# Gathering the experts' tokens as whole rows of 4 KB in two DMAs

## The chip, the cores and the metric

One core of one Trainium2 chip. The time is device microseconds of one execution. The engines are named as the profile names them: PE is TensorE (PEld its weight loads), DVE VectorE, ACT ScalarE, POOL GpSimd, SP SyncE.

## The reference, cut to what matters

The whole computation is an encoder block over 256 + 512 tokens of width 1024: a dilated attention beside a state-space mixer, then the expert layer, then a gated embedding. The change is in the expert layer:

```python
def _expert_choice_ffn(h, w_router, w_gate, w_up, w_down):   # h: (t, 1024), t = 512 and t = 256
    cap = max(1, CAPACITY_FACTOR * t // N_EXPERTS)           # 64 and 32 tokens an expert
    aff = jax.nn.softmax((h @ w_router).astype(jnp.float32), axis=-1)
    gate, idx = lax.top_k(aff.T, cap)                        # each of 16 experts chooses its tokens
    xs = h[idx]                                              # the gather
    def expert(args):
        xe, wg, wu, wd = args                                # (1024, 2816) twice, (2816, 1024)
        return (jax.nn.silu(xe @ wg) * (xe @ wu)) @ wd
    ye = lax.map(expert, (xs, w_gate, w_up, w_down)) * gate[..., None]
    return jnp.zeros_like(h).at[idx.reshape(-1)].add(ye.reshape(-1, h.shape[1]))   # the scatter
```

All of it is float32. The weights of 16 experts, 554 MB, are read once.

## The kernel before, in words

The kernel runs both groups of tokens (S, 512 of them; Q, 256) through the mixer and the router, then loops over 16 experts. An expert's 96 tokens stand in NB = 3 blocks of 32: two of S, one of Q.

**Layout of a block.** TensorE works in columns of 32: `blocks` (L1150) issues, for each block and each j of 0..3, a matmul with 32 stationary columns that writes 32 partitions of PSUM. The stationary operand of block b is `xts[e][b]`, 128 partitions x 256: partition 32 j + i holds features of the j-th quarter of a feature group, and the 32 columns of step k are the 32 tokens. To get there the normalized tokens are stored in DRAM (`hn_d`) with their features reordered in four quarters of 256 (L784), so that a quarter of a token is one run of 1 KB, row 4 t + j of `hn_d`.

**Gather and turn.** `quart` (L1108 to L1120) holds, for each block and expert, 128 row numbers 4 t + j. `gather(e)` (L1131) issues three indirect DMAs on POOL, one a block, each of which brings 128 runs of 1 KB to the 128 partitions of a buffer `xg0`, `xg1` or `xg2`. `turn_x(e)` (L1137) transposes each buffer in squares of 32 x 32 on DVE, 128x256 at once, into `xts`, which has two buffers a block. A buffer `xg` has one copy, so a gather waits until the transposes of the expert before have read it.

**The expert loop.** For each expert there are two halves r of the hidden width. `up(e, r)` (L1158) takes 16 weight tiles of 704 KB (gate and up in turn) into six PSUM banks, ACT and DVE evacuate them (`sg`, `hv`) and DVE transposes the result into `ht`. `down(e, r)` (L1173) takes 11 tiles of 512 KB. Their order is shifted: up(e,0), down(e-1,1), up(e,1), down(e,0), so that between two up phases there is always a down phase, in which the evacuation runs (but for the first expert, which has up(0,0) and up(0,1) back to back). After down(e,1) `emit` (L1205) scales with the gates and adds into DRAM with three indirect DMAs, the scatters. A scheduler that orders instructions by their dependences has put the transposes and the gather behind them at the evacuation of up(e,1), in the down phase of down(e,0), once an old `xts` is free.

**Weights.** `Feed` (L127) issues the 864 weight tiles on SP in the order of use into 25 slots; a slot is refilled when the last matmul on it is done, so SP waits for matmuls.

`PAD_L` and `PAD_R` are tiles that nothing uses: they set where in SBUF the pools behind them begin.

Of the kernel before, what the change touches and what calls it, by code (L numbers as in the profile page):

```python
# [10 lines left out]
F32 = mybir.dt.float32  # L11
BF16 = mybir.dt.bfloat16
F32R = mybir.dt.float32r
I32 = mybir.dt.int32
U32 = mybir.dt.uint32
AF = mybir.ActivationFunctionType
ALU = mybir.AluOpType
# [4 lines left out]
P = 128  # L22
D = 1024
# [8 lines left out]
NE = 16  # L32
CAPS = (64, 32)
NB = 3
FR = FF // 2
FC = FR // 4
DC = D // 4
# [129 lines left out]
def block_kernel(ctx, tc, x_prompt, x_sample, p_prompt, p_sample, rel_bias, g_mix, w_in, conv_w, conv_b, dt_bias,  # L167
                 a_log, d_skip, g_ssd, w_out, g_ffn, w_router, w_gate, w_up, w_down, g_pg, w_pg, w_ple, g_ple,
                 g_final, c_masks, c_table, c_rows, y_prompt, y_sample):
    nc, E = tc.nc, mybir.EngineType  # L170
    S, Q = Group(0), Group(1)

    def rows(prompt, sample, t):
        return prompt[t * P:(t + 1) * P, :] if t < 2 else sample[(t - 2) * P:(t - 1) * P, :]
# [1 line left out]
    x_rows = lambda t: rows(x_prompt[0], x_sample[0], t)  # L176
    p_rows = lambda t: rows(p_prompt[0, 0], p_sample[0, 0], t)
    N_B, N_C, N_D, PLE_A = 8, 11, 6, 4
    PAD_L, PAD_R = 88, 24
    y_rows = lambda t: rows(y_prompt[0], y_sample[0], t)  # L180

    def row_bcast(v, n):
# [2 lines left out]
    def pool(name, side):  # L185
        return tc.alloc_tile_pool(name=name, bufs=1, side=side, reuse_waits="tile")
# [36 lines left out]
    cpool = pool("consts", "left")  # L223
# [3 lines left out]
    dram = ctx.enter_context(tc.tile_pool(name="dram", bufs=1, space=DRAM))  # L227
    psum = ctx.enter_context(tc.tile_pool(name="psum", bufs=1, space=PSUM))

    def bank(tag, bufs):  # L230
        return psum.tile([P, 512], F32, tag=tag, bufs=bufs, name=tag)

    pA = lambda: bank("pA", 2)
    pB = lambda: bank("pB", 3)
# [5 lines left out]
    ident, u_le, u_ge, m_gt, m_lt, ones = (masks[:, i, :] for i in range(6))  # L240
# [6 lines left out]
    wr = cpool.tile([P, KD, NE], F32, name="wr")  # L247
    gates = cpool.tile([P, NB, NE], F32, name="gates")
    quart = cpool.tile([P, NB, NE], I32, name="quart")
    cpool.tile([P, PAD_L], F32, name="pad_l")  # L250

    tbl = dram.tile([H, 1024], F32, name="tbl")
    tbl_rep = dram.tile([H, P, 1024], F32, name="tbl_rep")
    for g in (S, Q):
        g.hn_d, g.acc_d = (dram.tile([4 * g.n, DC], F32, name=f"{x}{g.i}") for x in ("hn_d", "acc_d"))
        g.hn_rows, g.acc_rows = (x.rearrange("(t j) c -> t (j c)", j=4) for x in (g.hn_d, g.acc_d))


    latest, squares, halves_ = [], [], []
# [7 lines left out]
    def rstd_of(p, ss, n, width):  # L267
        r = p.tile([P, n], F32, tag="rstd", bufs=3, name="rstd")
        nc.vector.tensor_scalar(r, ss, 1.0 / width, EPS, op0=ALU.mult, op1=ALU.add)  # L269
        nc.gpsimd.tensor_tensor(r, r, mhalf[:, :n], op=ALU.pow)  # L270
        return r

    def sumsq(p, src, scr):
        ss = p.tile([P, 1], F32, tag="ss", bufs=3, name="ss")
        squares[:] = [nc.scalar.activation(scr, src, AF.Square, accum_out=ss)]
        return ss
# [759 lines left out]
    wk = pool("work", "right")  # L1036
# [6 lines left out]
    idx_u = wk.tile([32 + NE, CAPS[S.i]], U32, name="idxu")  # L1043
# [10 lines left out]
    at = pool("atts", "right")  # L1054
# [49 lines left out]
    sq, tq = slice(32, 32 + NE), slice(8 * FIRST_Q, 8 * ROUNDS)  # L1104
    p, p_q = pO(), pB()
    for u, x in enumerate((idx_u, vals)):
        reps = wk.tile([32 + NE, NB, 4, 32], F32, tag="reps", bufs=2, name="reps")
        nc.vector.tensor_copy(reps[:NE, :2], x[:NE].rearrange("p (b t) -> p b t", b=2).unsqueeze(2).to_broadcast(  # L1108
            [NE, 2, 4, 32]))
        nc.vector.tensor_copy(reps[sq, 2], x[sq, tq].unsqueeze(1).to_broadcast([NE, 4, 32]))  # L1110
        flat = reps.rearrange("p b j t -> p b (j t)")
        for b in range(2):
            nc.tensor.transpose(p[:, 32 * u + NE * b:32 * u + NE * (b + 1)], flat[:NE, b], ident[:NE, :NE])
        nc.tensor.transpose(p_q[:, NE * u:NE * (u + 1)], flat[sq, 2], ident[sq, sq])
        for y, src in ((slice(0, 2), p[:, 32 * u:32 * u + 32].rearrange("p (b e) -> p b e", b=2)),
                       (2, p_q[:, NE * u:NE * (u + 1)])):
            if u:
                nc.vector.tensor_copy(gates[:, y], src)
            else:
                nc.vector.tensor_scalar(quart[:, y], src, 4.0, rowc[:, 18:19], op0=ALU.mult, op1=ALU.add)  # L1120
    for _ in emb:
        pass
    w_a.release()
    w_c = pool("w_c", "left")
    exw = pool("experts", "left")
    of = (S, S, Q)
    xgs, xts, hts_, acc, pend = {}, {}, {}, {}, {}

    turned = []

    def gather(e):  # L1131
        xgs[e] = [exw.tile([P, DC], F32, tag=f"xg{b}", bufs=1, name="xg") for b in range(NB)]
        for b in range(NB):
            nc.gpsimd.indirect_dma_start(out=xgs[e][b], out_offset=None, in_=of[b].hn_d,  # L1134
                                         in_offset=bass.IndirectOffsetOnAxis(ap=quart[:, b, e:e + 1], axis=0))

    def turn_x(e):  # L1137
        xts[e] = [exw.tile([P, DC], F32, tag=f"x{b}", bufs=2, name="xe") for b in range(NB)]
        for b in range(NB):
            turned.append(nc.vector.transpose(xts[e][b], xgs[e][b]))  # L1140

    gather(0)
    wf.add(w_c, N_C)
    pw.release()
    w_d = pool("w_d", "right")
    wf.add(w_d, N_D)
    turn_x(0)


# [76 lines left out]
    for e in range(NE):  # L1226
        if e + 1 < NE:
            gather(e + 1)
        for r in range(2):
            up(e, r)  # L1230
            if r == 0 and e + 1 < NE:
                turn_x(e + 1)
                if 1 <= e <= NT:
                    ple_norm(e - 1)
            if e + r:
                down(e - 1 + r, 1 - r)
# [27 lines left out]
    for t in range(NT):  # L1264
        if t + 1 < NT:
            tail_prep(t + 1)
        xt, et, xh, xl, r = xs5.pop(t)
# [9 lines left out]
        r = rstd_of(wk, sumsq(wk, sg, q5.tile([P, D], BF16, tag="scr5", bufs=1, name="scr5")), 1, D)  # L1277
# [64 lines left out]
```

## Time and profile before

| | us |
|---|---|
| timed, median of 3 runs | 1941.67 |
| timed, lowest and highest | 1941.05, 1942.00 |
| profiled execution | 1953.96 |
| its span, first to last instruction | 1952.2 |
| PE busy in the span | 1908.5 |
| DVE, ACT, POOL busy | 476.2, 396.0, 280.4 |

The experts take the span from 476.5 us on (the first matmul of L1155) to 1862; before it are the mixer and router, behind it the gated embedding. In the page's 40 slices the DMA engines are at 9 of 10 from the tenth slice to the end of the experts and move 402 to 420 GB/s there; PE is at 9 throughout. Idle time of an engine that is not the bottleneck costs nothing, so the reading goes by what PE does from one half expert to the next. A line such as L1155 is the line of kernel.py that issued the instruction.

### The profile page before, as it was taken

To read this page: it belongs to the slowest core of one execution; us is meant where nothing else is said; L and a number is where in the kernel's file an instruction comes from. 1 tells how busy PE (TensorE), PEld (TensorE's weight loads), DVE (VectorE), ACT (ScalarE), POOL (GpSimd) and SP (SyncE) were. 2 spreads that over 40 slices of the span, in tenths; PEclk is the share of its full clock that TensorE was granted. 3 is DMA by queue.
4 is the path that set the end of the run, shared out by engine and by line. 5 is a ranking of instruction groups with operands and counts; after the bars stand their busy time and mean duration, and the time that the engine had idled before them with its cause. 6 is when DMAs were issued, how large, how long until landed. Compare 5 with 4: busy or idle time off the path is not lost.

```text
span 1952.2 us, 52796 instructions
## 1 busy us (share of the span) xinstructions
PE 1908.5 (98%) x23972; PEld 1525.3 (78%) x23972; DVE 476.2 (24%) x1002; ACT 396.0 (20%) x768; POOL 280.4 (14%) x278
## 2 busy tenths in 40 slices
PE   8999999998999999999999999999999999999988
PEld 7978988986688776788866668888888877777776
DVE  7767575735010000001100000010000000100144
ACT  6758645643000000000000000000000000000133
POOL 0342344222001011010101000010101000000110
PEclk9999999999999999999999999999999999999999
DMA  7553226267999999999999999999999999999821
GB/s 250 186 150 91 66 95 180 71 243 289 420 408 408 412 409 408 411 407 415 408 413 407 414 412 404 414 407 414 409 412 407 408 413 406 414 409 412 304 73 65
DMA packets 181601, 641.55 MB, mean 329 GB/s; under 512 B 21790, under 2 KB 56022, under 8 KB 181376
## 3 DMA queue, kind: packets, MB, share of 16 engines
q1 hardware_dynamic: 168108, 620.76, 79.9%
q0 software_dynamic: 13056, 17.31, 4.0%
q8 instruction: 188, 3.08, 0.6%
q14 instruction: 37, 0.30, 0.0%
q10 hardware_dynamic: 212, 0.09, 0.0%
HBM read 617.61 MB, written 19.96 MB: 327 GB/s over the span
## 4 chain that ended last, share of the span: by engine, by line
PE 90%; ACT 3%; DVE 3%; issue 2%; DMA 1%; POOL 0%; DVEq 0%; POOLq 0%; ACTq 0%
PE pA L1155 24%; PE pB L1155 23%; PE pT L1155 16%; PE pO L1155 8%; PE pA L263 5%; PE pA L264 5%; PE pA L265 5%; PE pO L702 2%; PE pT L693 1%; PE pT L281 1%; DVE ws L99 1%; DMA ws<-in_w_in 1%; ACT ws L98 1%; PE pB L790 0%; PE pB L685 0%
## 5 line engine op out<-in xcount | busy, mean ns | idle before, releaser
L1155 PE MATMUL pB<-wf,xe 128*32 128x352 f32 x6144 | 591.4, 460 | 6.0 <-DVE xe L1140 6.0
L1155 PE MATMUL pA<-wf,ht 128*32 128x256 f32 x8448 | 487.0, 379 | 3.1 <-issue 0.3
L1155 PEld LDWEIGHTS pA<-wf,ht 128*32 128x32 f32 x8448 | 395.3, 110 | 87.6 <-issue 20.4
L1155 PEld LDWEIGHTS pB<-wf,xe 128*32 128x32 f32 x6144 | 357.3, 110 | 118.2 <-DVE xe L1140 6.1
L1155 PE MATMUL pT<-wf,xe 128*32 128x352 f32 x4096 | 440.2, 460 | 0.0
L1170 DVE TENSOR_TENSOR hv<-sg,pT 128x352 f32<-128x352 f32 x64 | 32.1, 502 | 1232.7 <-PE pT L1155 1232.7
L1155 PEld LDWEIGHTS pT<-wf,xe 128*32 128x32 f32 x4096 | 244.7, 110 | 78.0 <-issue 2.2
L1155 PE MATMUL pO<-wf,xe 128*32 128x352 f32 x2048 | 287.1, 459 | 0.0
L1169 ACT ACTIVATE sg<-pB 128x352 f32<-128x352 f32 x96 | 44.6, 465 | 1091.2 <-PE pB L1155 1044.9
L1209 POOL DMA_INDIRECT acc_d<-ye,quart x48 | 75.5, 1574 | 730.4 <-ACT ye L1208 651.4
L1155 PEld LDWEIGHTS pO<-wf,xe 128*32 128x32 f32 x2048 | 131.3, 110 | 38.4 <-issue 0.4
L1134 POOL DMA_INDIRECT xg<-hn_d,quart x48 | 47.1, 981 | 300.9 <-DVE xe L1140 258.6
L99 DVE TENSOR_TENSOR ws<-ws 128x2048 fp32r<-128x2048 f32 (+1 forms) x31 | 68.5, 2214 | 39.2 <-ACT ws L98 38.8
L270 POOL TENSOR_TENSOR rstd<-rstd,mhalf 128x1 f32<-128x1 f32 (+1 forms) x36 | 22.9, 637 | 381.7 <-DVE rstd L269 381.7
L98 ACT ACTIVATE ws<-ws 128x2048 fp32r<-128x2048 f32 (+1 forms) x31 | 55.8, 1805 | 25.0 <-PE pA L264 13.0
L1208 ACT ACTIVATE ye<-pA,gates 128x256 f32<-128x256 f32 x48 | 19.4, 473 | 204.0 <-PE pA L1155 204.0
L265 PE MATMUL pA<-h,ws 128*128 128x512 f32 (+1 forms) x136 | 54.1, 398 | 1.2 <-DVE ws L99 1.2
L263 PE MATMUL pA<-h,ws 128*128 128x512 f32 (+1 forms) x136 | 54.7, 402 | 0.0
L264 PE MATMUL pA<-h,ws 128*128 128x512 f32 (+1 forms) x136 | 54.2, 398 | 0.0
L1171 DVE STREAM_TRANSPOSE ht<-hv 128x352 f32<-128x352 f32 x96 | 47.4, 519 | 0.6
L263 PE MATMUL pA<-wf,x 128*128 128x512 f32 x96 | 38.7, 403 | 6.7 <-ACT x L285 6.7
L263 PE MATMUL pA<-hq,ws 128*128 128x256 f32 (+1 forms) x136 | 40.0, 296 | 0.7 <-ACT xpq L382 0.7
(308 smaller groups left out, 2021.0 us busy)
## 6 DMA issues: line engine op xcount, KB each, us to landing
wf<-in_w_gate SPq DMA_DIRECT2D x256, 704.0 KB
wf<-in_w_up SPq DMA_DIRECT2D x256, 704.0 KB
wf<-in_w_down SPq DMA_DIRECT2D x352, 512.0 KB
ws<-in_w_in SPq DMA_DIRECT2D x24, 1024.0 KB
tbl_rep<-tbl SPq DMA_DIRECT2D x8, 512.0 KB
ws<-in_w_out SPq DMA_DIRECT2D x4, 1024.0 KB
wf<-in_w_pg SPq DMA_DIRECT2D x8, 512.0 KB
sk<-tbl_rep SPq DMA_DIRECT2D x8, 448.0 KB
```

Of the source, the lines that this page charges most:

```text
L98: self.nc.scalar.activation(hi, raw, AF.Copy)
L99: self.nc.vector.tensor_tensor(lo, raw, hi, op=ALU.subtract)
L263: nc.tensor.matmul(out, lhsT=sh, rhs=mh, start=first, stop=False)
L264: nc.tensor.matmul(out, lhsT=sh, rhs=ml, start=False, stop=False)
L265: latest[:] = [nc.tensor.matmul(out, lhsT=sl, rhs=mh, start=False, stop=last)]
L702: nc.tensor.matmul(po[:, c:c + HD], lhsT=pts[s - 3][j][:, k, :], rhs=g.v[:, k, h * HD:(h + 1) * HD], start=k == 0, stop=k == nt - 1)
L1134: nc.gpsimd.indirect_dma_start(out=xgs[e][b], out_offset=None, in_=of[b].hn_d, in_offset=bass.IndirectOffsetOnAxis(ap=quart[:, b, e:e + 1] ...
L1155: nc.tensor.matmul(out[b][32 * j:32 * j + 32], lhsT=st[b][:, 32 * k:32 * k + 32], rhs=w[:, j], start=first[b], stop=last, skip_group_check ...
L1169: nc.scalar.activation(sg, pg[b], AF.Silu)
L1170: nc.vector.tensor_tensor(hv, sg, pu[b], op=ALU.mult)
L1171: nc.vector.transpose(hts_[e, r][b], hv)
L1209: nc.gpsimd.indirect_dma_start(out=of[b].acc_d, out_offset=bass.IndirectOffsetOnAxis(ap=quart[:, b, e:e + 1], axis=0), in_=ye, in_offset=N ...
```

## The change

The tokens of experts 1 to 15 are fetched as whole rows of `hn_d` (4 KB a token) into one buffer `xg` of 128 x 1024, one token on a partition: rows 0 to 63 are the tokens of S, rows 64 to 95 those of Q. That takes two indirect DMAs, with the token numbers `token` as indices. The reordering in quarters that the three DMAs did is then done by the transposes: for block b and quarter j a 32x256 piece (partitions 32 b to 32 b + 31, columns 256 j on) goes to partitions 32 j to 32 j + 31 of `xts[e][b]`, four for each block, twelve for an expert. Expert 0 keeps the three DMAs by quarters and the three transposes, now into thirds of the same buffer's first 768 columns. `token` is made beside `quart`: the indices are cast to float (`ids`), transposed on PE and cast back. `hn_d` and `acc_d` are the same memory, declared by rows of 4 KB and viewed by quarters; the scatters are unchanged. `xg` grows from 3 KB to 4 KB a partition, and the pads are set anew.

```diff
-    PAD_L, PAD_R = 88, 24
+    PAD_L, PAD_R = 56, 88
...
+    token = cpool.tile([P, 2, NE], I32, name="token")
...
-        g.hn_d, g.acc_d = (dram.tile([4 * g.n, DC], F32, name=f"{x}{g.i}") for x in ("hn_d", "acc_d"))
-        g.hn_rows, g.acc_rows = (x.rearrange("(t j) c -> t (j c)", j=4) for x in (g.hn_d, g.acc_d))
+        g.hn_rows, g.acc_rows = (dram.tile([g.n, D], F32, name=f"{x}{g.i}") for x in ("hn_d", "acc_d"))
+        g.hn_d, g.acc_d = (x.rearrange("t (j c) -> (t j) c", j=4) for x in (g.hn_rows, g.acc_rows))
...
+    ids = wk.tile([32 + NE, CAPS[S.i]], F32, name="ids")
+    nc.vector.tensor_copy(ids[:NE], idx_u[:NE])
+    nc.vector.tensor_copy(ids[sq, :32], idx_u[sq, tq])
+    ps = pB(), pB()
+    nc.tensor.transpose(ps[0][:64, :NE], ids[:NE], ident[:NE, :NE])
+    nc.tensor.transpose(ps[1][:32, :NE], ids[sq, :32], ident[sq, sq])
+    for u, n in ((0, 64), (1, 32)):
+        nc.vector.tensor_scalar(token[:n, u], ps[u][:n, :NE], 1.0, None, op0=ALU.mult)
...
+    rows_of = ((S, slice(0, 64)), (Q, slice(64, 96)))
...
+    def fetch(out, src, at):
+        nc.gpsimd.indirect_dma_start(out=out, out_offset=None, in_=src,
+                                     in_offset=bass.IndirectOffsetOnAxis(ap=at, axis=0))
+
     def gather(e):
-        xgs[e] = [exw.tile([P, DC], F32, tag=f"xg{b}", bufs=1, name="xg") for b in range(NB)]
-        for b in range(NB):
-            nc.gpsimd.indirect_dma_start(out=xgs[e][b], out_offset=None, in_=of[b].hn_d,
-                                         in_offset=bass.IndirectOffsetOnAxis(ap=quart[:, b, e:e + 1], axis=0))
+        xgs[e] = exw.tile([P, D], F32, tag="xg", bufs=1, name="xg")
+        if e == 0:
+            for b in range(NB):
+                fetch(xgs[e][:, b * DC:(b + 1) * DC], of[b].hn_d, quart[:, b, e:e + 1])
+        else:
+            for g, r in rows_of:
+                fetch(xgs[e][r], g.hn_rows, token[:r.stop - r.start, g.i, e:e + 1])
 
     def turn_x(e):
         xts[e] = [exw.tile([P, DC], F32, tag=f"x{b}", bufs=2, name="xe") for b in range(NB)]
         for b in range(NB):
-            turned.append(nc.vector.transpose(xts[e][b], xgs[e][b]))
+            if e == 0:
+                turned.append(nc.vector.transpose(xts[e][b], xgs[e][:, b * DC:(b + 1) * DC]))
+                continue
+            for j in range(4):
+                turned.append(nc.vector.transpose(xts[e][b][32 * j:32 * j + 32], xgs[e][32 * b:32 * b + 32,
+                                                                                     j * DC:(j + 1) * DC]))
```

Three places of the built program show what moves. The first is DVE at a turn, the evacuation of up(e,1): `hv` is the product that empties two PSUM banks of a block, `ht` its transpose, `xe` the transposes of gathered tokens. Before:

```order
L1170 TENSOR_TENSOR hv<-sg,pT 128x352
L1140 STREAM_TRANSPOSE xe<-xg 128x256
L1171 STREAM_TRANSPOSE ht<-hv 128x352
L1170 TENSOR_TENSOR hv<-sg,pT 128x352
L1140 STREAM_TRANSPOSE xe<-xg 128x256 x2
L1170 TENSOR_TENSOR hv<-sg,pO 128x352
L1171 STREAM_TRANSPOSE ht<-hv 128x352 x2
```

DVE at the same place after the change:

```order
L1193 TENSOR_TENSOR hv<-sg,pT 128x352
L1162 STREAM_TRANSPOSE xe<-xg 32x256 x4
L1194 STREAM_TRANSPOSE ht<-hv 128x352
L1193 TENSOR_TENSOR hv<-sg,pT 128x352
L1162 STREAM_TRANSPOSE xe<-xg 32x256 x8
L1193 TENSOR_TENSOR hv<-sg,pO 128x352
L1194 STREAM_TRANSPOSE ht<-hv 128x352 x2
```

Every transpose of gathered tokens has become four, at the same places; the last `hv`, which empties bank pO, now has twelve of them ahead of it.

The second is POOL in the expert loop, with the semaphores each row waits for: a gather, the `rstd` of a norm, three scatters and the next gather. Before:

```order
L1134 DMA xg<-hn_d_87,quart 128x256 [waits DMASW0_49,DVE_49]
L270 TENSOR_TENSOR rstd<-rstd,mhalf 128x1 [waits DVE_49,Pool_49]
L1209 DMA acc_d_86<-ye,quart 2048x256 [waits DMAHW2_49,Activation_49]
L1209 DMA acc_d_88<-ye,quart 1024x256 [waits DMAHW6_49,DMAHW4_49,Activation_49]
L1209 DMA acc_d_86<-ye,quart 2048x256 [waits DMASW4_49]
L1134 DMA xg<-hn_d_85,quart 128x256 [waits DMASW1_49,DVE_49]
L1134 DMA xg<-hn_d_85,quart 128x256 [waits DMASW2_49,DVE_49]
L1134 DMA xg<-hn_d_87,quart 128x256 [waits DMASW3_49,DVE_49]
```

POOL at the same place after the change:

```order
L1142 DMA xg<-hn_d_88,token 32x1024
L271 TENSOR_TENSOR rstd<-rstd,mhalf 128x1 [waits DVE_49,Pool_49]
L1232 DMA acc_d_87<-ye,quart 2048x256 [waits DMASW3_49,Activation_49]
L1232 DMA acc_d_89<-ye,quart 1024x256 [waits DMASW2_49,Activation_49]
L1232 DMA acc_d_87<-ye,quart 2048x256 [waits DMASW6_49]
L1142 DMA xg<-hn_d_86,token 64x1024 [waits DMASW5_49,DMASW4_49,DVE_49]
L1142 DMA xg<-hn_d_88,token 32x1024
```

Three gathers, each of which waited for the transpose of its own buffer, have become two, of which the first waits for DVE and the second for nothing more.

The third is DVE between the choice of tokens and the first transposes of the experts. Before:

```order
L1108 CAST reps<-idxu 16x256
L1110 CAST reps<-idxu 16x128
L1108 COPY reps<-vals 16x256
L1110 COPY reps<-vals 16x128
L1120 TENSOR_SCALAR quart<-pO,rowc 128x32
L1120 TENSOR_SCALAR quart<-pB,rowc 128x16
L1118 COPY gates<-pO 128x32
L1118 COPY gates<-pB 128x16
L1140 STREAM_TRANSPOSE xe<-xg 128x256 x6
```

DVE there after the change:

```order
L1109 COPY reps<-vals 16x256
L1111 COPY reps<-vals 16x128
L1123 CAST ids<-idxu 16x64
L1124 CAST ids<-idxu 16x32
L1121 TENSOR_SCALAR quart<-pO,rowc 128x32
L1121 TENSOR_SCALAR quart<-pB,rowc 128x16
L1129 TENSOR_SCALAR token<-pB 64x16
L1129 TENSOR_SCALAR token<-pB 32x16
L1119 COPY gates<-pO 128x32
L1119 COPY gates<-pB 128x16
L1159 STREAM_TRANSPOSE xe<-xg 128x256 x3
L1162 STREAM_TRANSPOSE xe<-xg 32x256 x12
```

Two casts stand ahead of `quart`, on which the first gather waits, and the two `token` operations behind it.

## Rows read from the trace of the kernel before

**Rows 1.** The page: busy time by engine; the chain that ended last.

```profile
PE 1908.5 (98%) x23972; PEld 1525.3 (78%) x23972; DVE 476.2 (24%) x1002; ACT 396.0 (20%) x768; POOL 280.4 (14%) x278
...
PE pA L1155 24%; PE pB L1155 23%; PE pT L1155 16%; PE pO L1155 8%; PE pA L263 5%; PE pA L264 5%; PE pA L265 5%; PE pO L702 2%; PE pT L693 1%; PE pT L281 1%; DVE ws L99 1%; DMA ws<-in_w_in 1%; ACT ws L98 1%; PE pB L790 0%; PE pB L685 0%
```

**Rows 2.** Timeline of SP's queue: start, us, engine, line, op, out<-in.

```profile
1002.71 0.33 SPq L149 DMA_DIRECT2D wf<-in_w_up  x1
...
1006.26 0.33 SPq L149 DMA_DIRECT2D wf<-in_w_up  x1
```

**Rows 3.** Waits of SP's queue: us in total, times, longest us.

```profile
SPq L149 <- PE pO L1155: 287.4, 231, 1.4
```

**Rows 4.** Timeline of DVE: first `hv` after an up phase; idle before last.

```profile
535.06 0.52 DVE L1170 TENSOR_TENSOR hv<-sg,pT 128x352 f32<-128x352 f32 x1 [25.57 <-PE pT L1155]
...
1575.17 0.52 DVE L1170 TENSOR_TENSOR hv<-sg,pT 128x352 f32<-128x352 f32 x1 [39.83 <-PE pT L1155]
...
1619.28 0.52 DVE L1170 TENSOR_TENSOR hv<-sg,pT 128x352 f32<-128x352 f32 x1 [40.44 <-PE pT L1155]
...
1661.92 0.52 DVE L1170 TENSOR_TENSOR hv<-sg,pT 128x352 f32<-128x352 f32 x1 [39.83 <-PE pT L1155]
...
1704.57 0.52 DVE L1170 TENSOR_TENSOR hv<-sg,pT 128x352 f32<-128x352 f32 x1 [38.98 <-PE pT L1155]
```

**Rows 5.** Windows: busy us (instructions) by engine, clock, DMA share, GB/s.

```profile
883.00:885.00 2.00, 2.00 (x44) 1.56 (x39) 2.00 (x7) 0.00 (x0) 1.70 (x2) 1.00 1.02 425
885.00:887.00 2.00, 1.84 (x21) 0.53 (x13) 0.45 (x2) 0.00 (x0) 1.20 (x2) 1.00 1.01 411
887.00:889.00 2.00, 1.92 (x37) 1.63 (x39) 0.00 (x0) 0.00 (x0) 0.00 (x0) 1.00 1.02 419
...
1665.00:1667.00 2.00, 2.00 (x44) 1.79 (x37) 0.59 (x2) 0.00 (x0) 0.00 (x0) 1.00 1.01 422
```

**Rows 6.** Timeline of PEld in the first; idle before each in brackets.

```profile
885.71 0.17 PEld L1155 LDWEIGHTS pA<-wf,ht 128*32 128x32 f32 x4 [0.54 <-issue]
886.44 0.18 PEld L1155 LDWEIGHTS pA<-wf,ht 128*32 128x32 f32 x5 [0.56 <-issue]
887.17 0.83 PEld L1155 LDWEIGHTS pA<-wf,ht 128*32 128x32 f32 x19 [0.55 <-issue]
```

**Rows 7.** Waits of PEld: us in total, times, longest us.

```profile
PEld pA L1155 <- issue: 20.4, 38, 1.3
```

**Rows 8.** Timeline of POOL: gathers of that down phase.

```profile
882.93 1.03 POOL L1134 DMA_INDIRECT xg<-hn_d,quart  x1 [18.33 <-DVE xe L1140]
884.26 0.99 POOL L1134 DMA_INDIRECT xg<-hn_d,quart  x1 [0.30 <-issue]
```

**Rows 9.** Timeline of POOL: a scatter.

```profile
941.59 1.65 POOL L1209 DMA_INDIRECT acc_d<-ye,quart  x1 [11.67 <-ACT ye L1208]
```

**Rows 10.** Windows behind that scatter, as in rows 5.

```profile
943.00:945.00 2.00, 2.00 (x34) 1.76 (x28) 0.00 (x0) 0.00 (x0) 1.69 (x2) 1.00 1.02 406
945.00:947.00 2.00, 2.00 (x33) 1.76 (x29) 0.00 (x0) 0.00 (x0) 0.11 (x1) 1.00 1.06 378
```

**Rows 11.** DMA queues, 536 to 545 us: packets, MB, share of 16 engines.

```profile
q0 software_dynamic: 144, 0.39, 10.9%
```

**Rows 12.** DVE's groups by form: busy us, mean ns, idle before.

```profile
L1140 DVE STREAM_TRANSPOSE xe<-xg 128x256 f32<-128x256 f32 x48 | 19.4, 425 | 12.0 <-DMA xg<-hn_d,quart 12.0
```

**Rows 13.** Timeline of DVE at a turn: the last `hv`.

```profile
884.09 0.48 DVE L1170 TENSOR_TENSOR hv<-sg,pO 128x352 f32<-128x352 f32 x1
```

**Rows 14.** Timeline ahead of the first gather.

```profile
468.69 0.28 DVE L1108 CAST reps<-idxu 16x256 f32<-16x256 uint32 x1
469.00 0.22 DVE L1110 CAST reps<-idxu 16x128 f32<-16x128 uint32 x1
...
469.80 0.25 DVE L1120 TENSOR_SCALAR quart<-pO,rowc 128x32 int32<-128x32 f32 x1
...
470.34 1.08 POOL L1134 DMA_INDIRECT xg<-hn_d,quart  x1 [15.19 <-DVE quart L1120]
```

## The prediction, made before the result was known

> **What bounds the kernel now.** I read the page first: shares of the span and the chain that ended last [rows 1]. TensorE is busy 98% of 1952.2 us, and 71% of the span on that chain (24 + 23 + 16 + 8) are the expert matmuls of L1155. A busy TensorE may still be waiting for weights, so the next view was the queue of SyncE, which loads them. In steady state it issues one 704 KB tile every 1.775 us (two in 3.55) [rows 2], and its longest total of waits is for a matmul to free a slot [rows 3]. The slots hold 25 tiles, so a tile is asked for some 24 tiles, or over 30 us, before it is used. The experts go at the speed at which TensorE consumes tiles, and a transfer that is a few us late costs nothing.
>
> The third view is the start of the first `hv` after each half expert, a clock for TensorE. A half (16 up tiles and 11 down tiles) takes 42.64 or 42.65 us, and 44.11 us when a gather was issued in it (1575.17 to 1619.28, against 1619.28 to 1661.92 and 1661.92 to 1704.57) [rows 4]. The last of these is the telling one: it has the three transposes of a turn but no gather behind them, since no expert is left, and it is short. From 535.06 to 1661.92 there are 26 halves, 13 with a gather: 1126.86 - 26 x 42.645 = 18.1 us too long, 1.39 us a gather group. That is the largest sum in this trace that hangs on the gathers.
>
> [...] Weight loads stop three times for 0.54 to 0.56 us, between 885.2 and 887.2, and the profile calls the releaser "issue": nothing that it records was waited for [rows 6]. Over the run there are 38 such stops, 20.4 us, the longest 1.3 [rows 7]; 13 groups of three would be 39. The first of that group's three gathers was issued by GpSimd at 882.93, the next 1.33 us later [rows 8]. The stops come 2.3 to 4.3 us after the first.
>
> Scatters are software DMAs too, but beside a pair of them (941.59 and the one right behind it, in an up phase) the two stretches that lie 1.4 to 5.4 us behind it have 34 and 33 matmuls, no dip [rows 9, 10].
>
> **The change part by part.** The timed runs have a median of 1941.67 us, the profiled execution took 1953.96. I work out differences in the profiled execution and take them off the median. The 12.3 us between them are a doubt of their own, below.
>
> 1. Gathers of experts 3 to 15: three DMAs of 128 runs of 1 KB become two, of 64 and 32 rows of 4 KB, 393 KB as before. The bytes and packets lie beside weight transfers that are 24 tiles ahead: around a gather the software queue has 144 packets and 10.9% of the engines for 9 us [rows 11]. Whatever that becomes, it is hidden; without the tiles ahead it could give back at most 10.9% of 9 us = 1 us a group.
> What is not hidden are TensorE's stops. How two DMAs of whole rows stop it, no row shows. Bounds: none at all (the halves without a gather, 1.39 us saved, 18.1 us in 13 groups), and from the other side two stops of the longest kind in rows 7, 1.3 each, 2.6 us a group, 1.2 more than now, 15.7 us lost. There are three stops and three DMAs, so the nearest reading is one stop a DMA: two are left, 2/3 x 1.39 = 0.93 us, and 13 x 0.46 = 6.0 us are saved. I take that.
> 2. Transposes: twelve of 32x256 for three of 128x256 a turn. A transpose takes 425 ns [rows 12]; the columns are the same, so I put the narrow ones at that too, and nine more are 3.8 us of VectorE. They stand ahead of the last `hv` of the evacuation, which frees bank pO: after 884.09 + 0.48 = 884.6 [rows 13], with nine more after 888.4. TensorE wants pO again in the next up phase, behind 11 down tiles, 14.2 us (42.645 less 16 up tiles of 1.775), a gate tile and two thirds of an up tile, 17.2 us after the up phase ended near 881.8: at 899.0. Ten us of cover are left; cost 0. The cover is gone from (899.0 - 884.6) / 9 = 1.6 us for each added transpose, nearly four times the row. A gain is excluded: work is only added.
> 3. GpSimd: the first gather now waits for all twelve transposes (one buffer, not three) and is issued some 5 us later in the half (884.09 + 3.8 + 0.3 against 882.93); 2 instructions instead of 3. What it brings is transposed in the next turn, 86.75 us on (1575.17 to 1661.92) [rows 4]. Behind it in the queue stand the `rstd` of the embedding norm and the scatters, 40 and more us on. Cost 0.
> 4. Before the first gather VectorE has two more casts between the `reps` copies and `quart`, which gather(0) waits for and the first matmul behind it (`quart` at 469.80, the gather at 470.34) [rows 14]. The casts of `reps` there take 0.28 and 0.22 us for 256 and 128 columns; two of 64 and 32 columns cannot take more than 0.5 together, nor less than nothing; I take 0.4 us, near the rows, all on the path. The two extra transposes on TensorE and the `token` operations come behind what the gather needs: 0.
> 5. Gathers 1 and 2 run in the first up phase, beside matmuls that are less dense; a group of three becomes two, and the transposes of expert 1 end some 6 us later than now (3.8 of them, and a wait for all of gather 1). They are needed after the first down phase, 535.06 + 14.2 = 549 [rows 4], tens of us after they are issued. Cost 0.
>
> Sum: -6.0 + 0.4 = -5.6 us, so 1948.4 for a profiled execution and 1936.1 timed.
>
> [...]
>
> **The rivals.**
> - *The stop belongs to the group.* It starts 2.3 us after the first gather and the three stops are 0.73 us apart, while the gathers are 1.3 us apart [rows 6, 8]; so they may be no stop for each, but one burst that any gather sets off. Then nothing but point 4 is left: 1942.1. The same result follows if most of the stops are in the profiled execution alone: were all 12.3 us of the difference in them, the timed runs would hold 5.8 us, and two thirds of them left would save 1.9. [...]
> - *The stop goes altogether*, because it needs three DMAs in a row or many short runs; the pair of scatters that leaves no dip speaks for the first [rows 9, 10]. 18.1 - 0.4: 1924.0.
> - *The stop grows* (the other side): place, the down phase after each turn; the first DMA now moves 256 KB in 64 rows. If each of the two holds TensorE as long as the longest single stop, 1.3 us [rows 7], a group costs 2.6: +15.7 + 0.4, 1957.8. It decides against the change from 1.66 us a group (1.39 + 0.27; 13 x 0.27 + 0.4 = 3.9). Against it: fewer instructions and fewer runs.
> - *The transposes outlast their cover*: from 1.6 us each, on a row that says 0.43; at 2 us each, 9 x 0.4 = 3.8 us in each of 14 turns, +53. Counted with the case before.
>
> **How the numbers follow.** What a measurement of this kernel can tell from no change is about 0.2%, 3.9 us. The stops shrink with the DMAs or their runs: 0.40, 1936, own range 1928 to 1938. Gone: 0.12, 1924. The group's or the profile's: 0.36, 1942. Grown: 0.12, 1944 to 1958. Faster holds the first two but for the thin end of the first, 0.51; same 0.37; slower 0.12. The range goes from 1924, where the stops are gone, to 1946; beyond it lie most of the grown case and a little of the case without stops, some 0.13.
>
> **What would show it.** In the profile after, the halves with a gather against 42.645 us: 43.57 on the mean if I am right, 42.65 if the stops are gone, 44.0 if they belong to the group, over 44.3 if they grew; halves without one must stay at 42.64. TensorE's waits on "issue" in L1155's counterpart: two thirds of 20.4 us and of 38. The first matmul of the experts 0.4 us later. No wait of a matmul for a transpose or for an `hv`; one of over 1 us would prove point 2 wrong. If the half without a gather has changed, something that I did not see (the new places of tiles in memory) has moved TensorE's pace, and the forecast fails for a reason that no row of before shows.

## The result: slower, and held by the transfers

The changed kernel took 1957.45 us (median of 4 runs, 1956.86 to 1959.81), the kernel before beside it 1941.36 (1940.05 to 1942.00): ratio 1.0087, 95% interval 1.0075 to 1.0099. The forecast was 1936, with a range from 1924 to 1946. The changed kernel's profiled execution is one of these runs, 1956.86 us, span 1955.1.

### The profile after

The first view is again the start of the first `hv` behind each up phase, on DVE; for [rows 4].

```profile
1263.94 0.52 DVE L1193 TENSOR_TENSOR hv<-sg,pT 128x352 f32<-128x352 f32 x1 [34.41 <-PE pT L1178]
1306.58 0.52 DVE L1193 TENSOR_TENSOR hv<-sg,pT 128x352 f32<-128x352 f32 x1 [39.83 <-PE pT L1178]
1349.82 0.52 DVE L1193 TENSOR_TENSOR hv<-sg,pT 128x352 f32<-128x352 f32 x1 [35.00 <-PE pT L1178]
1393.22 0.52 DVE L1193 TENSOR_TENSOR hv<-sg,pT 128x352 f32<-128x352 f32 x1 [40.59 <-PE pT L1178]
```

From 538.98 to 1306.58 there are 18 halves of 42.64 or 42.65 us, with and without a gather: no stop of TensorE shows. (It need not be the change that took them away: the kernel before took 1941 us beside these runs, and its trace at 1940 us, b2 below, has none either.) From 1306.58 on the halves take 42.6 to 45.7 us, and halves without a gather are long as well. What they wait for stands in the waits of PEld from 1310 to 1600 us (total, times, longest):

```profile
PEld pB L1178 <- issue: 26.1, 134, 1.5
...
PEld pB L1178 <- DMA wf<-in_w_gate: 6.8, 17, 1.4
PEld pT L1178 <- DMA wf<-in_w_up: 6.1, 18, 1.0
PEld pA L1178 <- DMA wf<-in_w_down: 4.4, 6, 1.7
```

Weights come late: 41 waits, 17.3 us. The waits on "issue" are of 0.2 us mostly and begin with them; from 560 to 1300 the view is empty. The waits of SP's queue over the run, against [rows 3]:

```profile
SPq L149 <- DMA wf<-in_w_gate: 324.7, 225, 3.7
SPq L149 <- DMA wf<-in_w_up: 324.2, 231, 3.5
SPq L149 <- DMA wf<-in_w_down: 303.5, 331, 2.7
SPq L149 <- PE pB L1178: 50.6, 65, 5.8
```

The queue now waits for its own transfers (952 us; 240 before) and far less for a matmul to free a slot (136 us; 764 before). So the transfers are the bound. Where they lose is seen beside a gather: POOL's two gathers of one group, and windows of 2 us, the first of them 2 us behind the first gather, as [rows 5] (the last column is GB/s, the one before it the share of the DMA engines).

```profile
887.21 0.96 POOL L1142 DMA_INDIRECT xg<-hn_d,token  x1 [24.29 <-DVE xe L1162]
888.48 0.90 POOL L1142 DMA_INDIRECT xg<-hn_d,token  x1 [0.30 <-issue]
```

```profile
889.21:891.21 2.00, 2.00 (x45) 1.44 (x37) 0.00 (x0) 0.00 (x0) 0.17 (x1) 1.00 1.02 422
891.21:893.21 2.00, 2.00 (x44) 1.49 (x40) 0.00 (x0) 0.00 (x0) 0.00 (x0) 1.00 1.02 324
893.21:895.21 2.00, 2.00 (x41) 1.54 (x37) 0.00 (x0) 0.00 (x0) 0.00 (x0) 1.00 1.02 289
895.21:897.21 2.00, 2.00 (x33) 1.08 (x28) 0.00 (x0) 0.00 (x0) 0.00 (x0) 1.00 1.01 406
```

The last column falls from 422 to 324 and 289 GB/s while the DMA engines stay as busy (1.01 to 1.02): the packets take longer. The weight packets of 5.6 KB, 215 ns each just before, took 285 and 308 on the mean in the two windows from 891.21 on. At a gather of the kernel before it stayed at 411 to 425 [rows 5]. Against 420 the three windows lack (96 + 131 + 14) x 2 us = 0.48 MB, 1.15 us of all transfers. With 14 steady groups (experts 2 to 15) that is 16 us of transfers. The whole loop says the same: from 538.98 to the last such `hv` at 1828.89 the weights' queue moved 394.4 GB/s (508.75 MB), in b2 399.4; at b2's rate the same bytes take 16.0 us less.

Not all of the 16 us come out as time. The halves are 10.6 us too long in sum (11.2 to 12.1 in a2, a3 and a4); the other 5.4 us are 2.2 MB more than in b2 that were taken from the tiles ahead, and 1.9 us of them show behind the last `hv` (126.2 us to the end, 124.3 in b2). That is 12.5 us. The rest of the 16.5 between the two spans, 4.0, stands before the first `hv` (538.98 against 534.96), where other executions differ as much (533.75 in e7b, 539.84 in e8b) and where point 4 of the prediction has 1.0.

Why so small a loss, early in the run, shows only at 1306 us: over 600 to 1250 us the weights' queue moved (packets, MB, share of 16 engines) in the changed kernel

```profile
q1 hardware_dynamic: 57212, 254.94, 97.0%
```

392.2 GB/s. TensorE consumes 17.30 MB in 42.645 us, 405.7 GB/s. The 13.5 GB/s between them come out of the tiles ahead. Counted from 538.98 to 1306.58, the queue moved 301.92 MB and 18 halves used 311.43: 9.5 MB. The 25 slots hold 16 MB (864 tiles, 554 MB) at the most, and part of that is always on its way: 13.5 us from issue to landing, at this rate 5.3 MB (an estimate). So the lead is used up there, and what is lost later is a wait.

### The profile page after: what moved, and what is told of

It is laid out like the page before. It is cut to its first block, busy times and chain, and to the rows that moved or that the text cites. A ratio compares the mean times of both kernels' runs of the same rounds, so it can differ in the third digit from the quotient of the medians.

```text
span 1955.1 us, 52897 instructions
## 1 busy us (share of the span) xinstructions
PE 1901.8 (97%) x23974; PEld 1228.1 (63%) x23974; DVE 540.9 (28%) x1141; ACT 396.2 (20%) x768; POOL 264.9 (14%) x263
## 5 line engine op out<-in xcount | busy, mean ns | idle before, releaser
L1178 PE MATMUL pB<-wf,xe 128*32 128x352 f32 x6144 | 600.0, 461 | 10.6 <-DVE xe L1159 6.8
L1178 PE MATMUL pA<-wf,ht 128*32 128x256 f32 x8448 | 476.2, 379 | 8.2 <-DMA wf<-in_w_down 8.0
L1178 PE MATMUL pT<-wf,xe 128*32 128x352 f32 x4096 | 447.9, 461 | 0.9 <-DMA wf<-in_w_up 0.9
L1178 PEld LDWEIGHTS pA<-wf,ht 128*32 128x32 f32 x8448 | 320.1, 110 | 161.1 <-DMA wf<-in_w_down 15.5
L1178 PEld LDWEIGHTS pB<-wf,xe 128*32 128x32 f32 x6144 | 258.6, 110 | 231.8 <-issue 60.5
L1178 PE MATMUL pO<-wf,xe 128*32 128x352 f32 x2048 | 293.8, 459 | 0.0
L1178 PEld LDWEIGHTS pT<-wf,xe 128*32 128x32 f32 x4096 | 182.8, 110 | 155.3 <-issue 38.6
L1192 ACT ACTIVATE sg<-pB 128x352 f32<-128x352 f32 x96 | 44.5, 463 | 1086.0 <-PE pB L1178 1039.6
L1178 PEld LDWEIGHTS pO<-wf,xe 128*32 128x32 f32 x2048 | 107.3, 110 | 75.7 <-issue 21.9
L1162 DVE STREAM_TRANSPOSE xe<-xg 32x256 f32<-32x256 f32 x180 | 78.2, 435 | 10.1 <-DMA xg<-hn_d,token 7.6
L1142 POOL DMA_INDIRECT xg<-hn_d,token x30 | 27.6, 920 | 359.6 <-DVE xe L1162 349.3
## 6 DMA issues: line engine op xcount, KB each, us to landing
wf<-in_w_gate SPq DMA_DIRECT2D x256, 704.0 KB, 13.5
wf<-in_w_up SPq DMA_DIRECT2D x256, 704.0 KB, 13.5
wf<-in_w_pg SPq DMA_DIRECT2D x8, 512.0 KB, 10.2
```

Of the source, the lines that this page charges most:

```text
L1142: nc.gpsimd.indirect_dma_start(out=out, out_offset=None, in_=src, in_offset=bass.IndirectOffsetOnAxis(ap=at, axis=0))
L1162: turned.append(nc.vector.transpose(xts[e][b][32 * j:32 * j + 32], xgs[e][32 * b:32 * b + 32, j * DC:(j + 1) * DC]))
L1178: nc.tensor.matmul(out[b][32 * j:32 * j + 32], lhsT=st[b][:, 32 * k:32 * k + 32], rhs=w[:, j], start=first[b], stop=last, skip_group_check ...
L1192: nc.scalar.activation(sg, pg[b], AF.Silu)
```

## The experiments

The experiments ran in five groups, each on a chip of its own with the kernel before beside it. That kernel comes in two levels, 1955 us on two chips (14 and 12) and 1941 on the other three (10, 1 and 6) and beside the result; each comparison is with the kernel before on the same chip.

**Other partitions for the same rows.** e1 puts S on partitions 32 to 95 and Q on 0 to 31, e2 S on 64 to 127. The transposes follow; instructions and order are the same.

```diff
-    rows_of = ((S, slice(0, 64)), (Q, slice(64, 96)))
+    rows_of, base = ((S, slice(32, 96)), (Q, slice(0, 32))), (32, 64, 0)      # e2: S 64 to 127, Q 0 to 31, (64, 96, 0)
...
-                turned.append(nc.vector.transpose(xts[e][b][32 * j:32 * j + 32], xgs[e][32 * b:32 * b + 32,
+                turned.append(nc.vector.transpose(xts[e][b][32 * j:32 * j + 32], xgs[e][base[b]:base[b] + 32,
```

The loss was 1.15 us a group. A theory that the expectations call 'halves' puts it down to gathered rows that lie on one half of the partitions alone, 0 to 63 or 64 to 127, as S and Q do in the changed kernel (324 and 289 GB/s, the dip); it was a guess of mine, which e1 and e2 were to try.

Expected of e1:

> The changed kernel with other places for the gathered rows and nothing else: S on partitions 32 to 95, Q on 0 to 31. [...] Then the S part of the dip goes (two thirds of the rows) and the Q part stays: about 0.4 us a group, 1957.5 - 14 x 0.7 = 1947 us. Rival 'rows': runs of 4 KB are slow wherever they land: the dip stays, 1957. Rival 'pads': the new places of the weight slots make all transfers slower: 1957.

Expected of e2:

> The changed kernel with S on partitions 64 to 127 and Q on 0 to 31. 'Halves': S is on one half again, only the other one, so the dip of the changed kernel stays, 1957 us. 'Rows' and 'pads': 1957 too. A third theory, that partitions 0 to 31 are slow for a reason of their own (something else lives there): only Q's rows are left on them, 1947 or less.

Measured: e1 1944.69 us, e2 1956.67, the kernel before 1955.03; ratios 0.9953 (0.9940 to 0.9967) and 1.0009 (1.0000 to 1.0018). On one chip, by nothing but the partitions, e1 is 12.0 us faster than e2. Windows 4 us behind the first gather of a group, e1:

```profile
889.27:891.27 2.00, 2.00 (x44) 1.53 (x37) 0.00 (x0) 0.00 (x0) 0.00 (x0) 1.00 1.00 404
891.27:893.27 2.00, 2.00 (x44) 1.57 (x40) 0.00 (x0) 0.00 (x0) 0.00 (x0) 1.00 1.05 355
```

and e2:

```profile
888.68:890.68 2.00, 2.00 (x44) 1.56 (x39) 0.00 (x0) 0.00 (x0) 0.00 (x0) 1.00 1.05 335
890.68:892.68 2.00, 2.00 (x43) 1.51 (x36) 0.00 (x0) 0.00 (x0) 0.00 (x0) 1.00 1.03 291
```

With S on 32 to 95 little is left of the first dip (404 GB/s, where the changed kernel has 324 and e2 335), and the second (355) is put down to Q's rows on 0 to 31; with S on the upper 64 it is that of the changed kernel (335 and 291 against 324 and 289). It is the partitions that count, not rows of 4 KB, and not the low partitions as such. These placements, and the one over all 128 partitions in e8 below (415 and 417), agree with 'halves'. How rows on one half slow the transfers beside them is not shown.

**Without the gathers, without the scatters.** e4 leaves out the gathers of experts 3 to 15 (their tokens are expert 2's), e5 the scatters of experts 0 to 14, both in the kernel before.

```diff
-        xgs[e] = [exw.tile(...) for b in range(NB)]  # e4, in gather
-        for b in range(NB):
+        xgs[e] = xgs[2] if e > 2 else [exw.tile(...) for b in range(NB)]
+        for b in range(NB if e < 3 else 0):
...
-            nc.gpsimd.indirect_dma_start(            # e5, in emit
+            e == NE - 1 and nc.gpsimd.indirect_dma_start(
```

Expected of e4:

> The kernel before without the gathers of experts 3 to 15 (their tokens are those of expert 2; the transposes stay). In the profile all theories want every half at 42.65 us and an execution of 1953.96 - 18.1 = 1936 us. Timed: 1936 if TensorE sets the end; if the transfers set it even without 13 groups of gathers, more, up to 1941.

Expected of e5:

> The kernel before without the scatters of experts 0 to 14 (the gathers stay). The transfers gain some 20 us of slack. If the timed kernel before (1941.4) is held by its transfers, and TensorE's stops at the gathers are in profiled executions alone: 1936 timed, about 1953 profiled. If the stops are there without a profile and what the timed runs show is their sum: 1941 timed, 1953 profiled.

Measured beside the same 1955.03: e4 1939.28 us (0.9917, 0.9904 to 0.9931), e5 1960.41 (1.0025, 1.0015 to 1.0036). In e4 all halves but two late ones are 42.64 or 42.65. In e5 the stops stand as in the kernel before (gather halves 43.7 to 44.5) though its transfers had slack (SP's queue waited 987 us for matmuls to free slots and under 11 for any kind of weight tile to land; from 560 to 1700 us PEld waited on "issue" alone, 18.8 us in 33 stops): where the kernel before takes 1955, it is by TensorE's stops and not by its transfers. Neither of the times expected of e5 came. That it was 5 us slower came mostly from behind the loop: from the last first `hv` to the end it took 125 us, the traced kernel before 120. I did not follow it further.

**The two kernels again, elsewhere.** b2 is the kernel before, a2 the changed one.

Expected of b2:

> The kernel before, unchanged, for a trace that belongs to its time. It took 1941.4 us where the changed kernel took 1957.5, and 1955.0 beside the last four runs. If the difference is TensorE's stops at the gathers: a time near 1955 goes with 13 halves of about 44.1 us, a time near 1941 with gather halves of 42.7 to 43.0. If it is elsewhere: 44.1 in both.

Expected of a2:

> The changed kernel, unchanged, beside the kernel before in the same place. It is held by its transfers from some 1300 us on, and these don't depend on TensorE's stops: 1957 us, as the first time, whether the kernel before takes 1941 or 1955 here. If whatever makes the kernel before differ from place to place moves the changed one as well: up to 1971 or down to 1943.

Measured: b2 1940.34 us (one run; the 15 beside it 1941.40), a2 1955.08, ratio 1.0071 (1.0058 to 1.0085). Two gather-and-no-gather halves of b2, then the end of the loop:

```profile
876.12 0.52 DVE L1170 TENSOR_TENSOR hv<-sg,pT 128x352 f32<-128x352 f32 x1 [37.30 <-PE pT L1155]
918.77 0.52 DVE L1170 TENSOR_TENSOR hv<-sg,pT 128x352 f32<-128x352 f32 x1 [38.98 <-PE pT L1155]
961.41 0.52 DVE L1170 TENSOR_TENSOR hv<-sg,pT 128x352 f32<-128x352 f32 x1 [37.30 <-PE pT L1155]
...
1814.31 0.52 DVE L1170 TENSOR_TENSOR hv<-sg,pT 128x352 f32<-128x352 f32 x1 [39.83 <-PE pT L1155]
```

All 30 halves are 42.64 or 42.65: here the kernel before has no stops at all, three gathers of 128 runs or not. Its weights' queue from 600 to 1250 us:

```profile
q1 hardware_dynamic: 58175, 259.01, 97.5%
```

398.5 GB/s, 7.2 less than TensorE consumes. From 534.96 to 1814.31 the queue moved 510.92 MB and 30 halves used 519.05: 8.1 MB of its lead are gone at the end of the loop, where the changed kernel began to wait at 9.5. The kernel before just gets through on its lead; in its last down phase matmuls do wait for down tiles, 2.4 us in sum.

**The gathers twice.** e9 issues each gather of the changed kernel twice.

```diff
-            for g, r in rows_of:
+            for g, r in rows_of + rows_of:
```

Expected:

> The changed kernel with every gather of experts 1 to 15 issued twice into the same buffer. 'Halves': twice the dip, 1.1 us a group, and 0.39 MB more at 418 GB/s, 0.94 us a group, both on the transfers that set the end: 1956 + 14 x 2.0 = 1984. If the loss of the changed kernel comes from its transposes, its order or its places in memory and not from the gathers: the bytes alone, 1956 + 13 = 1969 at most.

Measured: 1989.85 us (before 1955.32; 1.0177, 1.0162 to 1.0193), some 34 us over the changed kernel on other chips (1955 to 1957): 13 for the bytes, and 21 left for a dip that cost 16 the first time. In its trace the second pair of a group, issued 8.4 us behind the first (at 895.31), dips once more, to 297 and 273 GB/s. Its halves grow long from 880 us on, not 1306. The loss goes with the gathers; its size came out 6 us over what was expected.

**Half rows over all partitions.** e6 and e8 fetch S as 128 half rows of 2 KB, Q as 128 runs of 1 KB: two DMAs over all 128 partitions, nine transposes. They differ in 60 B of padding in a small table, which moves all that lies behind it: in e8 it lies where the changed kernel has it, in e6 60 B lower.

```diff
+            fetch(xgs[e][:, :2 * DC], S.hn_rows.rearrange("t (h c) -> (t h) c", h=2), token[:, e:e + 1])
+            fetch(xgs[e][:, 2 * DC:], Q.hn_d, quart[:, 2, e:e + 1])
...
+    hrow = cpool.tile([P, 1], F32, name="hrow")              # in e6
+    hrow = cpool.tile([P, 16], F32, name="hrow")[:, :1]      # in e8, in its place
```

Expected of e6:

> S gathered as 128 half rows of 2 KB, one on each partition, Q as 128 runs of 1 KB as in the kernel before: two DMAs, both over all 128 partitions; eight transposes of 32x256 and one of 128x256. 'Halves': no dip of the transfers at a gather (410 GB/s and more), no wait for weights. TensorE's stops, if they go by the number of runs (384 a group: 1.39 us, 96: 0.2): 256 runs, 0.9 us, 1951 us where the kernel before takes 1955. If they go by the gather's place in the half (later, behind the added transposes): under 0.3 us a group, 1941 to 1943. 'Rows': a dip half as deep, some 0.5 us a group, hidden.

Expected of e8:

> The half rows again (S 128 half rows of 2 KB, Q 128 runs of 1 KB), with the small tables padded so that everything behind them in memory lies where the changed kernel has it (in the run before it lay 60 B lower, and its weight packets of 4 KB took 164 ns instead of 162 in stretches without a gather, 411.7 GB/s instead of 414 to 415). 'Halves' and the shift of 60 B as the cause of the slow weights: no dip at the gather, 414 to 415 GB/s elsewhere, no wait for weights: 1940 to 1943 where the kernel before takes 1941. If the half rows themselves cost the transfers: 1956 again.

And of e8 and e1 again in other places:

> The half rows with the padded tables again: 1942 where the kernel before takes 1955, and where it takes 1941: 1940 to 1943, the same as it, since nothing stops TensorE there.

> The kernel with S on partitions 32 to 95 and Q on 0 to 31 again, in a place of its own. Where the kernel before takes 1955 (TensorE stopping at its gathers): 1944.7 as the first time. Where it takes 1941 (no stops): 'halves' has only Q's dip left, about 0.35 us a group, which the lead of the weights covers: 1941 to 1944, not faster than the kernel before. A cost in rows of 4 KB as such: 1955.

Measured: e6 1956.73 us beside a kernel before of 1941.40 (1.0078, 1.0064 to 1.0091). e8 1942.61 and e1b 1943.69 beside 1955.32 (0.9936, 0.9922 to 0.9950; 0.9946, 0.9933 to 0.9960); e8b 1943.91 beside 1941.15 (1.0011, 1.0001 to 1.0020). e8 behind its gather:

```profile
888.74:890.74 2.00, 2.00 (x44) 2.00 (x39) 0.00 (x0) 0.00 (x0) 0.00 (x0) 1.00 1.02 415
890.74:892.74 2.00, 2.00 (x44) 2.00 (x39) 0.00 (x0) 0.00 (x0) 0.00 (x0) 1.00 1.03 417
```

No dip, and it takes 1942 to 1944 on either chip. On one chip e8b is 11.4 us faster than the changed kernel (a3, below, 1955.30): the loss of the change is repaired but for 2.8 us against the kernel before there, and what is gained over the kernel before is only the stops, where there are any. e6 had no dip either and was as slow as the changed kernel, which I had not expected; its weights' queue from 600 to 1250 us, and e8's:

```profile
q1 hardware_dynamic: 57641, 256.95, 97.3%
```

```profile
q1 hardware_dynamic: 58174, 259.02, 97.5%
```

395.3 against 398.5 GB/s (398.9 in e8b); e6's halves stay at 42.65 to 1562.98 and then wait for weights, with 10.2 MB of the lead used. 60 B in the place of the slots go with 3.2 GB/s, and the lead again decided when that showed. e6 and e8 ran on different chips, and e6 was not run again, so that the 60 B are the cause is likely, not shown; the kernel before on e6's chip (b2) moved 398.5.

**The transposes alone.** e7 is the kernel before with four 32x256 transposes for each of 128x256; its gathers stay.

```diff
-            turned.append(nc.vector.transpose(xts[e][b], xgs[e][b]))
+            [turned.append(nc.vector.transpose(xts[e][b][i:i + n], xgs[e][b][i:i + n]))
+             for n in (32 if e else P,) for i in range(0, P, n)]
```

Expected, of the first run and of two more:

> The kernel before with its transposes alone changed: each of 128x256 becomes four of 32x256 on the same buffers (experts 1 to 15); the gathers stay three DMAs of 1 KB runs, issued some 4 us later. If transposes cost TensorE nothing and the stops go by runs or DMAs: same as before, gather halves 44.1 us (where the kernel before has them). If the stops come from the gather's place beside the evacuation: gather halves 42.65 to 43, up to 17 us less than before. If transposes hold up a bank: halves over 44.5.

> The kernel before with its transposes alone changed (four of 32x256 for each of 128x256, gathers of three DMAs of 1 KB runs, some 4 us later), again, for a place where the kernel before takes 1955 and TensorE stops at its gathers, which there were none of the first time. If the stops go by runs or DMAs: gather halves of 44.0 to 44.1 us, 1955, same as before. If they come from the gather's place beside the evacuation: 42.7 to 43.1, 1941 to 1944. Where the kernel before takes 1941: 1941, and the question stays open.

> The kernel before with the twelve narrow transposes alone, once more for a place with stops. Where the kernel before takes 1955: 44.0 to 44.1 us a gather half and 1955 if the stops go by runs or DMAs, 42.7 to 43.1 and 1941 to 1944 if they come from the gather's place. Where it takes 1941: 1941, and the question is left open.

Measured: 1940.71, 1941.47 and 1940.71 us beside 1941.40, 1941.15 and 1940.83; 0.9999 (0.9990 to 1.0009), 1.0003 (0.9994 to 1.0012), 1.0000 (0.9990 to 1.0009). All halves are 42.64 or 42.65. The transposes cost nothing that shows; on the stops the three runs say nothing, since none fell where there are any.

**The changed kernel beside these.** Expected:

> The changed kernel again. Its transfers set its end: 1955 to 1958 wherever it runs; against a kernel before that takes 1955 it is no slower (ratio 1.000 to 1.002), against one of 1941 slower by 0.8%.

> The changed kernel, once more: 1955 to 1958 wherever it runs. Where the kernel before takes 1955, gather halves up to 1300 us of 42.65 to 43.1 (the stops mostly gone) and a ratio of 1.000 to 1.002; where it takes 1941, 42.65 and 1.007.

Measured: 1955.30 and 1956.52 us, 1.0070 (1.0057 to 1.0084) and 1.0076 (1.0059 to 1.0093). It never ran beside a kernel before of 1955; the nearest is e2, 1.0009 there.

## Why the prediction was wrong

- *The bound.* The step that failed is in the first paragraph and again in point 1: "a transfer that is a few us late costs nothing", "Whatever that becomes, it is hidden". A lead hides a late transfer only if it is refilled. Here the queue delivered 398.5 GB/s against 405.7, so the 24 tiles ahead were being used up from the first expert on, and most of what the transfers lost was due before the end: of 16 us some 12 (12.0 from e2 to e1, 11.4 from a3 to e8b, 12.5 in the halves and behind them in the changed kernel's trace). [Rows 3] hid this: in that execution TensorE's own stops had slowed consumption to 17.30 MB in 43.34 us, 399.2 GB/s, so that SP waited for matmuls. In b2, without stops, SP's longest waits are its transfers (289.2 us for up tiles; 85.8 is its longest total for matmuls).
- *Point 1, the cost.* "It could give back at most 10.9% of 9 us = 1 us a group" had the right size for the share of the packets, and the sign wrong: the new gathers took 1.15 us a group more from the transfers, 16 us. Bytes and packets were as counted; what I left out was where they land, 64 and 32 partitions in place of 128. e1, e2 and e8 show that this is the cause; e9 bears out the size but for 5 to 6 us.
- *Point 1, the gain.* The 18.1 us of stops were measured rightly. That gathers like the new ones are nearly free of them is shown on the two chips where the kernel before takes 1955: 0.2 us a group in e1, e1b and e8, and as much in e2 while its weights are in time. The four traces of the changed kernel itself show none, but beside a kernel before that has none either. And the timed 1941.67 belonged, by its level, to executions that had none: b2 took 1940.34 without a stop. The 12.3 us between profile and timed runs, which I called a doubt, were then these stops, 18.1 us in the halves less 4.6 that came back behind the last `hv` (119.7 us to the end, against 124.3 in b2); taking the difference off the timed median credited them a second time. It is the rival of the stops that are in the profile alone, told wrongly (they come with the chip, or with what else differed between the groups of runs), and it gave 1942.1, near what e8b, without the loss, shows (1943.91).
- *Why the stops go* is open. By the number of runs it is not: e8 has 256 a group and its gather halves are 0.17 us over 42.645 on the mean, e1 has 96 and 0.21, the kernel before 384 and 1.39. No run shows, then, that a quarter of the stops would stay with a quarter of the runs, which gave the 1928 at the low end of the first case. By the number of DMAs in a group it is hardly: e9 has four, two and two, on a chip where the kernel before takes 1955, and its four gather halves up to 880 us take 42.65, 42.96, 42.65 and 42.99. Three DMAs right behind one another, or their earlier issue beside the transposes, are left; e7 was to tell and could not.
- *Point 2* held: a narrow transpose took 435 ns (425 assumed), and the last `hv` of a turn ended 7.4 us after the start of the first (6.6 forecast, 881.78 to 888.4); once the experts' loop ran, no matmul waited for either. In the rival of the transposes 9 x 0.4 is 3.6, not 3.8, and its price 50 us, not 53; nothing hung on it. The rows of that turn, on DVE:

```profile
880.13 0.52 DVE L1193 TENSOR_TENSOR hv<-sg,pT 128x352 f32<-128x352 f32 x1 [37.30 <-PE pT L1178]
880.57 1.78 DVE L1162 STREAM_TRANSPOSE xe<-xg 32x256 f32<-32x256 f32 x4
...
883.36 3.58 DVE L1162 STREAM_TRANSPOSE xe<-xg 32x256 f32<-32x256 f32 x8
886.97 0.52 DVE L1193 TENSOR_TENSOR hv<-sg,pO 128x352 f32<-128x352 f32 x1
```

- *Point 4* was too small: from the first `reps` cast to the first gather 1.65 us before [rows 14] and 2.61 after, 0.96 for 0.4.

```profile
470.45 0.28 DVE L1109 CAST reps<-idxu 16x256 f32<-16x256 uint32 x1
...
471.54 0.18 DVE L1123 CAST ids<-idxu 16x64 f32<-16x64 uint32 x1
471.75 0.17 DVE L1124 CAST ids<-idxu 16x32 f32<-16x32 uint32 x1
471.95 0.25 DVE L1121 TENSOR_SCALAR quart<-pO,rowc 128x32 int32<-128x32 f32 x1
...
472.26 0.23 DVE L1129 TENSOR_SCALAR token<-pB 64x16 int32<-64x16 f32 x2
```

```profile
473.06 1.09 POOL L1142 DMA_INDIRECT xg<-hn_d,quart  x1 [16.15 <-issue]
```

The two casts took 0.41 as assumed, but `quart` to gather went from 0.54 to 1.11 us: the gather now came after the `token` operations, which I had put behind what it needs. The trace names no releaser, so that it waited for them is likely, not shown.
- *The rival of the other side* gave slower, but by TensorE's stops growing. The mechanism that came, transfers slowed by where a gather lands, was not among the rivals.

## What to carry to other kernels

A lead in a queue is a stock: compare what the queue delivers with what is consumed (here 398.5 GB/s against 405.7), and if it delivers less, a loss of the transfers is paid in the end, however early it is and however far ahead the tiles seem, but for what is left of the stock (here some 12 of 16 us were paid). When a DMA's shape changes at the same bytes, look at which partitions it lands on: here 64 rows astride 64 left 404 GB/s and on either half 324 and 335, which was 12.0 us of the whole between e1 and e2, and all 128 partitions left 415. And where a profiled execution and the timed runs differ by more than the effect that is hunted, find what differs before taking a saving off the timed number.

## What the runs showed of the hardware

- A gather of 0.39 MB onto 64 and 32 partitions pulled what the core's DMA engines move from 422 to 324 and 289 GB/s for 4 us, the weights' transfers with it (their packets of 5.6 KB took 285 and 308 ns, 215 before; changed kernel); onto all 128 it left 415 and 417 (e8), and the 64 on partitions 32 to 95 left 404 (e1).
- TensorE's stops beside the same gathers (1.39 us a group, "issue") are there in one trace of the kernel before (and in e5, on a chip where it takes 1955) and absent in another (b2, where it takes 1941). The cause was not found.
- Moving the weight slots by 60 B went with 395.3 in place of 398.5 and 398.9 GB/s, and with 13 to 14 us, in a kernel that lives on its lead (e6 against e8 and e8b, on different chips).
